# A two-layer attention, convolution and MLP trunk in split fp32: softmax scalings on VectorE, a new start condition for normalisations, and a margin ahead of attention's TensorE steps

## The chip, the cores and the metric

One NeuronCore of a Trainium2 chip runs the whole program. The metric is the device time of one execution in microseconds, as the median of several runs. TensorE has two clock levels here, 1.2 and 2.4 GHz; the profile gives the granted clock of a stretch as a share of the full one.

## The reference

Latent tokens (512) and context tokens (256) of width 1024 pass through two layers. Everything is fp32. Cut to what matters:

```python
for l in range(DEPTH):                                   # 2 layers
    h = rms_norm(x, g_norm1[l]) * (1 + sc1) + sh1        # shifts and scales: silu(c) @ w_mod + b
    na_q, na_k, na_v, cv_x, cv_b, cv_c, wa_q, wa_k, wa_v = split_proj(h @ w_in[l])
    o_na = neighborhood_attention(...)                   # 4 heads, 8 x 16 window, position bias
    o_cv = cv_b * short_conv(cv_c * cv_x, ...)           # depthwise, 3 taps
    o_wa = window_attention(...)                         # 8 heads, +-128 tokens, sink logits, rotary
    x = x + gt1 * (concat(rms_norm(o_na), rms_norm(o_cv), rms_norm(o_wa)) @ w_o[l])
    x = x + gt2 * (square(relu((rms_norm(x, g_norm2[l]) * (1 + sc2) + sh2) @ w_fc1[l])) @ w_fc2[l])
```

Both attentions are a softmax over the 256 context keys and the local keys together: `p = exp(s - max) / sum`, then `p @ v`. The context tokens go through the same steps, with a softmax over themselves, in layer 0; in layer 1 only their keys and values are needed.

## The kernel before, in words

**Tiling.** Activations lie transposed, 128 channels in the partitions and up to 768 tokens (512 latent, 256 context) along the free axis; `xs[k]` holds channels 128k to 128k+127. A product is computed to nearly fp32 by splitting each operand into a high part in fp32r and a low rest: for each step of 128 channels three matmuls add high weight times high activation, high times low and low times high into one PSUM bank `psmm` (`steps`, 526). A weight chunk arrives by DMA as `wraw`, is copied to `whi`, and the rest `wraw - whi` becomes `wlo` (`weights`, 493). In the trace `hh`/`hl` are the split activations behind a normalisation, `oh`/`ol` those of the attention outputs, `gh`/`gl` those within the MLP.

**Order.** A Python planner writes the program. Each piece of work is a generator ("stream") with a priority, run by `_Order.run` (from 280). A stream yields either a condition or a planned time, and is resumed when this has come. Each call of an engine goes through `_Engine.__getattr__` (one line, L206, which therefore stands in every row of the trace): `_cost` (209) gives a planned duration, and `_Model.op` finds the first gap in the engine's planned timetable. VectorE work whose wide operands all lie in SBUF and all GpSimd work also take a place in one common timetable called port. At the end `emit` issues all calls in order of planned start, and that is the order in which each engine does them. `quickest` (464) chooses between engines: the one with the earliest planned end plus a given penalty. `copy` chooses between ScalarE and VectorE, `minus`, `plus` and `times` between GpSimd and VectorE.

**Attention.** `attention_streams` (716) runs three streams per layer. `scores` makes logits, maxima and exponentials; `exp_norm` (698) does the exponential on ScalarE with its row sum, the reciprocal `sm` on VectorE, and then scales the probabilities `pb` (latent) or `pbc` (context) in place by `sm`, by `quickest` between GpSimd and VectorE. `transposes` (831) waits for the scaled tile by `yield md.at(pb)` and transposes it on TensorE into `pst` or `pstc`, from where `split_pt` makes `pth` and `ptl`. `products` (892) waits by `yield md.at(pth, ptl)` and multiplies with the values into `pso`. Matmuls of other streams (the remaining input projections, the output projection) fill TensorE between.

**Normalisations.** `norm` (601) computes the row statistic (`psr`, `t`, `acc`) and then, for each of the eight channel tiles, `tn` (VectorE), `hh` (ScalarE) and `hl` (VectorE). `group` (1090) does the same for an output group: `o` on VectorE, then the split into `oh` and `ol`. Ahead of each tile both wait in `room` (594) for a time that the planner finds.

Both layers run: modulation, norm, input projection with attention beside it, group normalisations, output projection, norm, fc1, squared ReLU, fc2. `x<-psmm` rows add a product to the residual. In layer 1 the second half of the program works on latent tokens in two segments of 256.

Of the kernel before, what the change touches and what calls it, by code (L numbers as in the profile page):

```python
# [10 lines left out]
AF = mybir.ActivationFunctionType  # L11
# [31 lines left out]
NBEG = (2, 3)  # L43
NTO = (2, 3)
NT = 2
SLACK = 3000.0


B_HI, B_LO, B_SM, B_SC = 100.0, 400.0, 700.0, 4000.0
NG = 18  # L50
NL, NS = 6, 3
SEM = 170.0
# [129 lines left out]
class _Engine:  # L182
# [26 lines left out]
    def _cost(self, op, n, outs, ins, k):  # L209
        if self._name == "PE":  # L210
            part, self._md.part = self._md.part, (ins[0].shape[0] > 64, outs[0].shape[0] > 32)
            c = 0.0 if part == self._md.part else 190.0
            if op == "transpose":
                return c + 109.0
            if ins[0].dtype == F32R:
                return c + max(n / 2.4 + 13.6, 110.0)
            return c + (4 * n / 2.4 if outs[0].shape[0] > 32 else 105.0)
        if self._name == "DMA":
            return outs[0].shape[0] * n * 4 / 360.0
        scalars = sum(1 for x in ins if x.shape[1:] == (1,) or list(x.shape[1:]) == [1]) if n > 1 else 0  # L220
        if self._name == "Activation":
            acc = 93.0 if k.get("accum_out") is not None else 0.0
            return (52.0 if ins[0].space == bass.MemoryType.PSUM else 93.0) + 0.8333 * n + 93.0 * scalars + acc
        if self._name == "Pool":
            return 149.0 + (2.104 if op == "tensor_tensor" else 0.9) * n
        if op == "reciprocal":
            return 69.0 + 6.25 * n
        return 69.0 + (0.52 if op == "tensor_scalar" else 1.0417) * n + 61.0 * min(scalars, 1)
# [85 lines left out]
def hybrid_trunk(ctx: ExitStack, tc: tile.TileContext, a: dict, out: bass.AP):  # L314
# [276 lines left out]
        copy(hi, t)  # L591
        minus(lo, t, hi.bitcast(F32))

    def room():

        yield md.start_of("DVE", 600.0) - 700.0

    def norm_tiles():
        return [[hp.tile([P, T], F32R, name=nm, tag="h") for _ in range(KC)] for nm in ("hh", "hl")]
# [1 line left out]
    def norm(l, which, xs, acc, hs, ls, s, seg, ready, end):  # L601

        s0, s1 = seg
        yield from row_rstd(acc, s0, s1, D)
        sh = M_SH1 if which == 0 else M_SH2
        for k in range(KC):
            yield f_mod[l, 2 * which, k // 4]
            yield from room()
            t = tmp("tn")
            b = modc[l][:, sh + k, s:s + 1]  # L610
            vec.scalar_tensor_tensor(out=t[:, s0:s1], in0=xs[k][:, s0:s1], scalar=amod[l][:, which, k, s:s + 1],
                                     in1=acc[:, s0:s1], op0=ALU.mult, op1=ALU.mult)
            act.activation(hs[k][:, s0:s1], t[:, s0:s1], AF.Identity, bias=b)
            hi = hs[k][:, s0:s1].bitcast(F32)
            vec.scalar_tensor_tensor(out=ls[k][:, s0:s1], in0=t[:, s0:s1], scalar=b, in1=hi, op0=ALU.add,
                                     op1=ALU.subtract)
            if k == 0:
                ready.set()
        if end:
            free(acc)  # L620
# [77 lines left out]
    def exp_norm(dst, src, mn, sink, tail=0):  # L698

        sm = ap_.tile([P, 2], F32, name="sm", tag="sm", bufs=6)  # L700
        act.activation(dst, src, AF.Exp, bias=mn, scale=-1.0, accum_out=sm[:, 0:1])
        if sink is not None:
            act.activation(sm[:, 1:2], sink, AF.Exp, bias=mn, scale=-1.0)
            vec.tensor_tensor(out=sm[:, 0:1], in0=sm[:, 0:1], in1=sm[:, 1:2], op=ALU.add)
        vec.reciprocal(sm[:, 0:1], sm[:, 0:1])
        w = dst.shape[1] - tail
        k = {"out": dst[:, 0:w], "in0": dst[:, 0:w], "scalar1": sm[:, 0:1], "scalar2": None, "op0": ALU.mult}
        quickest((pool, "tensor_scalar", (), k, 0.0), (vec, "tensor_scalar", (), k, B_SM))

    def split_pt(pt, n, dh, dl):  # L710
        src = pt[:, :P * n].rearrange("p (c q) -> p c q", c=dh.shape[1])
# [4 lines left out]
    def attention_streams(l, last, units, o_done):  # L716
# [114 lines left out]
        def transposes():  # L831
            pts = None
            done = 0
            while done < total:
                yield lambda: to_t
                un, j, pair, b, pb = to_t.pop(0)
                yield md.at(pb)
                if pair == 2 or b % 2 == 0:
                    yield r_pt.need()
                    r_pt.take()  # L840
                    pts = (ap_.tile([P, PTW], F32R, name="pth", tag="pth"),
                           ap_.tile([P, PTW], F32R, name="ptl", tag="ptl"))
                pth, ptl = pts
                whole = [x[:, 0:1024].rearrange("p (s q) -> p s q", s=4) for x in pts]
                half = [x[:, 1024:PTW].rearrange("p (s q) -> p s q", s=1) for x in pts]
                if pair == 2:
                    yield r_ps.need()
                    r_ps.take()
                    pt = psp.tile([P, 512], F32, name="pstc", tag="ps")
                    for c in range(2):  # L850
                        for b in range(2):
                            pe.transpose(pt[:, 256 * c + P * b:256 * c + P * b + P],
                                         pb[:, 256 * b + P * c:256 * b + P * c + P], ident)
                    split_pt(pt, 4, whole[0][:, 0:2, :], whole[1][:, 0:2, :])
                    r_ps.give(md.last(pt))
                else:

                    if un["u"] < 2:
                        parts = (([(128, 256, 384)], 0, 64), ([(0, 256, 384, 128)], 0, None),
                                 ([(0, 256, 384, 128)], 0, None), ([(0, 128, 256)], 1, 384))[b]  # L860
                        parts = [(cs, parts[1]) for cs in parts[0]] + ([parts[2]] if parts[2] is not None else [])
                    else:
                        parts = ([((256, 384, 0, 128), 0)], [((0, 128, 384, 512), 0), ((256,), 4)],
                                 [((128, 384, 512, 256), 0), ((0,), 4)], [((0, 256, 384, 128), 0)])[b]
                    qo = P * (b % 2)
                    for part in parts:
                        if isinstance(part, int):

                            pe.transpose(pt[0:64, 384:512], pb[:, part:part + 64], ident)
                            ph = 64 * pair  # L870
                            dh = pth[ph:ph + 64, 1024:PTW]
                            act.activation(dh, pt[0:64, 384:512], AF.Copy)
                            vec.tensor_tensor(out=ptl[ph:ph + 64, 1024:PTW], in0=pt[0:64, 384:512],
                                              in1=dh.bitcast(F32), op=ALU.subtract)
                            r_ps.give(md.last(pt))
                            continue
                        cs, s0 = part
                        n = len(cs)
                        yield r_ps.need()
                        r_ps.take()  # L880
                        pt = psp.tile([P, 512], F32, name="pst", tag="ps")
                        for i, c in enumerate(cs):
                            pe.transpose(pt[:, P * i:P * i + P], pb[:, c:c + P], ident)
                        split_pt(pt, n, *(half if s0 == 4 else [x[:, s0:s0 + n, qo:qo + P] for x in whole]))
                        if part is parts[-1] or not isinstance(parts[-1], int):
                            r_ps.give(md.last(pt))
                r_pb.give(md.last(pb))
                if pair == 2 or b % 2 == 1:
                    to_pv.append((un, j, pair, pth, ptl))
                    done += 1  # L890

        def products():
            for _ in range(total):
                yield lambda: to_pv
                un, j, pair, pth, ptl = to_pv.pop(0)
                yield md.at(pth, ptl)
                yield r_ps.need()
                r_ps.take()
                v, o, h0, u = un["v"][j], un["o"], 64 * j, un["u"]
# [65 lines left out]
    def main():  # L965
# [16 lines left out]
        for l in range(DEPTH):  # L982
# [107 lines left out]
            def group(gi, os_, base, n, flags, f):  # L1090
# [8 lines left out]
                for (s0, s1) in segs:  # L1099
                    yield from row_rstd(acc, s0, s1, n)  # L1100
                    for i, o in enumerate(os_):
                        if s0 == 0:
                            yield r_g.need(2)
                            r_g.take(2)
                            oh[base + i] = gp.tile([P, T], F32R, name="oh", tag="g")
                            ol[base + i] = gp.tile([P, T], F32R, name="ol", tag="g")
                        yield from room()
                        vec.scalar_tensor_tensor(out=o[:, s0:s1], in0=o[:, s0:s1], scalar=vc(V_GO + base + i),
                                                 in1=acc[:, s0:s1], op0=ALU.mult, op1=ALU.mult)
                        split(oh[base + i][:, s0:s1], ol[base + i][:, s0:s1], o[:, s0:s1])  # L1110
# [283 lines left out]
```

## Time and profile before

| | |
|---|---|
| median of 3 runs | 1689.58 us (1686.2 to 1690.01) |
| profiled execution | 1685.32 us |
| its span | 1683.5 us |
| mean granted TensorE clock | 0.986 |
| busy: TensorE, VectorE, ScalarE, GpSimd | 1590.3 (94%), 982.0 (58%), 694.9 (41%), 290.4 us (17%) |
| moved by DMA | 182.25 MB, 108 GB/s on average |

The span is the time from the first to the last instruction that the profiler recorded in one execution. Layer 0's attention lies at about 40 to 322 us and layer 1's at about 1045 to 1258 us; the rest is mostly dense products. A row that ends in `[4.57 <-DVE wlo L206]` says that the engine stood idle for 4.57 us before this instruction, and that VectorE's `wlo` ended the wait. PE is TensorE, PEld its weight loads, DVE VectorE, ACT ScalarE, POOL GpSimd.

### The profile page before, as it was taken

Reading aid. Unit: us, or ns where it says so; the run is one execution under the profiler, and the core shown is the slowest. Engines: PE = TensorE matmul, PEld = TensorE weight load, DVE = VectorE, ACT = ScalarE, POOL = GpSimd, SP = SyncE. Lnnn points to the kernel's source line nnn. Section 1 sums busy time; section 2 is a strip of 40 time slices with the busy share of each in tenths; the row PEclk is TensorE's granted clock in tenths of the full one; section 3 lists DMA queues with packets and bytes.
Section 4 is the critical chain, followed back from the end, with each engine's and each line's share of the span. In section 5 each row is a group of like instructions: output and inputs, shape, how many; then the busy total and the mean of one; then the engine's idle time right before and its main releaser. Section 6 shows DMA issues by size and latency. Waiting matters only on the chain. (4 is left out here: it accounts for less than half of the span.)

```text
span 1683.5 us, 24437 instructions
## 1 busy us (share of the span) xinstructions
PE 1590.3 (94%) x9210; PEld 1310.3 (78%) x9210; DVE 982.0 (58%) x1956; ACT 694.9 (41%) x1385; POOL 290.4 (17%) x287
## 2 busy tenths in 40 slices
PE   5999999998899999999999998988999899999999
PEld 1777778777688888888888877777778788888887
DVE  4798888855643334234334457887886754545353
ACT  3667776534431122113113345656764532323231
POOL 1034666300000000000000001356752000000000
PEclk8999999999999999999999998999999999999999
DMA  9332311245433233333321233311214322322222
GB/s 325 105 112 82 126 60 52 91 162 173 145 121 123 103 126 111 115 120 106 126 94 62 88 129 116 92 51 57 53 62 136 120 97 97 100 91 100 98 98 102
DMA packets 75719, 182.25 MB, mean 108 GB/s; under 512 B 9425, under 2 KB 15825, under 8 KB 75601
## 3 DMA queue, kind: packets, MB, share of 16 engines
q1 hardware_dynamic: 75600, 180.69, 32.7%
q8 instruction: 72, 1.18, 0.3%
q14 instruction: 47, 0.38, 0.1%
HBM read 170.43 MB, written 5.24 MB: 104 GB/s over the span
## 5 line engine op out<-in xcount | busy, mean ns | idle before, releaser
L206 PE MATMUL psmm<-hh,whi 128*128 128x512 f32 (+1 forms) x1264 | 459.5, 363 | 4.0 <-ACT hh L206 3.6
L206 PE MATMUL psmm<-hl,whi 128*128 128x512 f32 (+1 forms) x1264 | 445.1, 352 | 1.3 <-DVE hl L206 0.8
L206 PE MATMUL psmm<-hh,wlo 128*128 128x512 f32 (+1 forms) x1264 | 443.9, 351 | 0.0
L206 ACT ACTIVATE whi<-wraw 128x512 fp32r<-128x512 f32 x319 | 199.6, 629 | 442.1 <-PE psmm L206 421.0
L206 DVE TENSOR_TENSOR wlo<-wraw,whi 128x512 fp32r<-128x512 f32 x370 | 259.3, 705 | 133.1 <-ACT whi L206 129.2
L206 PE MATMUL psmm<-gh,wlo 128*128 128x512 f32 (+1 forms) x768 | 273.3, 356 | 10.3 <-DVE wlo L206 10.3
L206 PEld LDWEIGHTS psmm<-hh,whi 128*128 128x128 f32 x1264 | 240.3, 190 | 51.6 <-issue 18.5
L206 PE MATMUL psmm<-gh,whi 128*128 128x512 f32 (+1 forms) x768 | 276.4, 360 | 0.0
L206 PE MATMUL psmm<-gl,whi 128*128 128x512 f32 (+1 forms) x768 | 273.2, 356 | 0.0
L206 PEld LDWEIGHTS psmm<-hh,wlo 128*128 128x128 f32 x1264 | 240.1, 190 | 32.5 <-DVE wlo L206 0.2
L206 PEld LDWEIGHTS psmm<-hl,whi 128*128 128x128 f32 x1264 | 240.7, 190 | 30.9 <-DVE hl L206 3.6
L206 DVE SCALAR_TENSOR_TENSOR x<-psmm,modc,x 128x512 f32<-128x512 f32 (+1 forms) x96 | 63.5, 661 | 197.0 <-PE psmm L206 196.9
L206 POOL TENSOR_SCALAR pb<-pb,sm 128x512 f32<-128x512 f32 (+2 forms) x96 | 159.6, 1667 | 101.2 <-DVE sm L206 90.9
L206 PEld LDWEIGHTS psmm<-gh,wlo 128*128 128x128 f32 x768 | 146.5, 191 | 31.0 <-DVE wlo L206 10.5
L206 PEld LDWEIGHTS psmm<-gh,whi 128*128 128x128 f32 x768 | 146.5, 191 | 29.2 <-issue 10.1
L206 PEld LDWEIGHTS psmm<-gl,whi 128*128 128x128 f32 x768 | 146.5, 191 | 19.6 <-issue 0.2
L206 ACT ACTIVATE rl<-psmm 128x512 f32<-128x512 f32 (+1 forms) x98 | 50.9, 519 | 256.8 <-PE psmm L206 256.4
L206 DVE TENSOR_TENSOR sqf<-rl 128x512 f32<-128x512 f32 (+1 forms) x98 | 58.2, 594 | 156.1 <-ACT rl L206 152.8
L206 POOL TENSOR_TENSOR acc<-acc,sq 128x256 f32<-128x256 f32 x33 | 27.3, 827 | 680.8 <-ACT sq L206 680.5
L206 PE MATMUL psmm<-oh,wlo 128*128 128x256 f32 (+1 forms) x256 | 81.3, 318 | 9.6 <-DVE wlo L206 9.6
L206 PE MATMUL pst<-ident,pb 128*128 128x128 f32 (+1 forms) x416 | 64.9, 281 | 26.1 <-POOL pb L206 25.2
L206 PE MATMUL psmm<-oh,whi 128*128 128x256 f32 (+1 forms) x256 | 83.8, 327 | 3.6 <-ACT oh L206 3.6
(141 smaller groups left out, 2140.1 us busy)
## 6 DMA issues: line engine op xcount, KB each, us to landing
wraw<-in_w_fc SPq DMA_DIRECT2D x134, 512.0 KB, 3.5
wm<-in_w_mod SPq DMA_DIRECT2D x192, 256.0 KB, 4.2
wraw<-in_w_in SPq DMA_DIRECT2D x33, 512.0 KB, 3.5
wraw<-in_w_o SPq DMA_DIRECT2D x27, 512.0 KB, 3.6
tb<-in_namask SPq DMA_DIRECT2D x24, 256.0 KB, 2.8
sw<-qg SPq DMA_DIRECT2D x40, 64.0 KB, 2.0
kl<-kl SPq DMA_DIRECT2D x12, 192.0 KB, 2.6
x<-in_xT SPq DMA_DIRECT2D x8, 256.0 KB, 5.2
```

The costliest lines, as they stand in the source:

```text
L206: self._md.log.append((s, len(self._md.log), lambda: f(*a, **k)))
```

## The change

The scaling of probabilities is now chosen between VectorE, without a penalty, and ScalarE, with a penalty of 9999 ns. The planner's cost of a GpSimd `tensor_scalar` is 277 + 2.504 ns a column in place of 149 + 0.9. `room` is given the statistic's tile and asks for the first gap that the coming instruction would really have, after its input is ready, on VectorE and the port timetable, less 700 ns; before it asked for the first 600 ns gap on VectorE from the planner's present time on, less 700 ns. The two TensorE streams of attention are resumed 400 ns after their data is planned to be there.

```diff
+LATE = 400.0
...
-B_HI, B_LO, B_SM, B_SC = 100.0, 400.0, 700.0, 4000.0
+B_HI, B_LO, B_SM, B_SC, B_RM = 100.0, 400.0, 9999.0, 4000.0, 700.0
...
         if self._name == "Pool":
-            return 149.0 + (2.104 if op == "tensor_tensor" else 0.9) * n
+            return 149.0 + 2.104 * n + (128.0 + 0.4 * n if op == "tensor_scalar" else 0.0)
...
-    def room():
-
-        yield md.start_of("DVE", 600.0) - 700.0
+    def room(x):
+
+        yield md.slot("DVE", max(md.t, md.ready(x, "DVE", False)), 69.0 + 61.0 + 1.0417 * x.shape[1], [x]) - B_RM
...
-            yield from room()
+            yield from room(acc[:, s0:s1])
...
-        quickest((pool, "tensor_scalar", (), k, 0.0), (vec, "tensor_scalar", (), k, B_SM))
+        quickest((vec, "tensor_scalar", (), k, 0.0), (act, "activation", (dst[:, 0:w], dst[:, 0:w], AF.Copy),
+                                                      {"scale": sm[:, 0:1]}, B_SM))
...
-                yield md.at(pb)
+                yield md.at(pb) + LATE
...
-                yield md.at(pth, ptl)
+                yield md.at(pth, ptl) + LATE
```

The second `room` call, in `group`, is changed in the same way. Counted over the program, 120 scalings go from GpSimd to VectorE (48 of 512 columns, 32 of 640, 16 of 448, 24 of 256) and none to ScalarE; 13 `wlo` go from VectorE to GpSimd, and 36 small copies from VectorE to ScalarE. TensorE's and the DMA queue's instructions keep their number.

In layer 0's attention, VectorE's list around one unit's maxima `mn_350` and reciprocal `sm_351` before:

```order
L206 ISA pb_349,mn_350<-sc_348,wamask_111,sinks_108 128x512
L206 ISA mn_350 128x1
L206 TENSOR_TENSOR ptl_344<-pst_352,pth_343 128x4x128
L206 TENSOR_TENSOR ptl_344<-pst_353,pth_343 128x128
L206 RECIPROCAL sm_351<-sm_351 128x1
L206 TENSOR_REDUCE mnc_356<-scc_354 128x2
```

and with the change (line 206 is now 207; the numbers name the tiles):

```order
L207 ISA pb_349,mn_350<-sc_348,wamask_111,sinks_108 128x512
L207 ISA mn_350 128x1
L207 TENSOR_TENSOR ptl_344<-pst_355,pth_343 128x4x128
L207 TENSOR_TENSOR ptl_344<-pst_356,pth_343 128x128
L207 RECIPROCAL sm_351<-sm_351 128x1
L207 TENSOR_SCALAR pb_349<-pb_349,sm_351 128x512
```

The scaling of `pb_349` now stands behind the reciprocal in VectorE's own list.

At the end of layer 0, where layer 1's first normalisation (`tn`, `hl`) meets the last fc2 products of layer 0 (`x`) and the next weights, VectorE's list before:

```order
L206 SCALAR_TENSOR_TENSOR tn<-x_1146,amod_115,acc 128x512
L206 SCALAR_TENSOR_TENSOR hl<-tn,modc_113,hh 128x512 x2
L206 SCALAR_TENSOR_TENSOR tn<-x_1157,amod_115,acc 128x512
L206 SCALAR_TENSOR_TENSOR tn<-x_1168,amod_115,acc 128x512
L206 SCALAR_TENSOR_TENSOR hl<-tn,modc_113,hh 128x512 x2
L206 SCALAR_TENSOR_TENSOR x_1126<-psmm,modc_112,x_1126 128x256
L206 TENSOR_TENSOR wlo<-wraw,whi 128x512
L206 SCALAR_TENSOR_TENSOR x_1135<-psmm,modc_112,x_1135 128x256
```

and with the change:

```order
L207 SCALAR_TENSOR_TENSOR x_1132<-psmm,modc_112,x_1132 128x256
L207 TENSOR_TENSOR wlo<-wraw,whi 128x512
L207 SCALAR_TENSOR_TENSOR tn<-x_1106,amod_115,acc 128x512
L207 SCALAR_TENSOR_TENSOR x_1143<-psmm,modc_112,x_1143 128x256
L207 TENSOR_TENSOR sq<-x_1143 128x256
L207 SCALAR_TENSOR_TENSOR hl<-tn,modc_113,hh 128x512
L207 TENSOR_TENSOR wlo<-wraw,whi 128x512
L207 SCALAR_TENSOR_TENSOR x_1154<-psmm,modc_112,x_1154 128x256
L207 TENSOR_TENSOR wlo<-wraw,whi 128x512
L207 SCALAR_TENSOR_TENSOR tn<-x_1109,amod_115,acc 128x512
```

The block of pairs is broken up: weight rests and residual sums stand between `tn` and `hl`, and the later pairs come behind them.

At the end of layer 1's attention, where `o_2537` is the fourth tile of the window-attention group and `acc_2489` (now `acc_2491`) the statistic of the last group, before:

```order
L206 SCALAR_TENSOR_TENSOR t_2726<-psr_2725,t_2726 128x512
L206 SCALAR_TENSOR_TENSOR acc_2489<-t_2726,acc_2489 128x512
L206 SCALAR_TENSOR_TENSOR o_2354<-o_2354,vecs_91,acc_2489 128x512
L206 SCALAR_TENSOR_TENSOR o_2619<-o_2619,vecs_91,acc_2489 128x512
L206 TENSOR_TENSOR ol_2728<-o_2354,oh_2727 128x512
L206 TENSOR_TENSOR ol_2730<-o_2619,oh_2729 128x512
L206 SCALAR_TENSOR_TENSOR o_2537<-o_2537,vecs_91,acc_2312 128x512
```

and with the change:

```order
L207 TENSOR_TENSOR wlo_2726<-wraw_2672,whi_2725 128x512
L207 SCALAR_TENSOR_TENSOR o_2537<-o_2537,vecs_91,acc_2303 128x512
L207 TENSOR_TENSOR ol_2723<-o_2537,oh_2722 128x512
L207 TENSOR_TENSOR ocv_2731<-psmm_2724,y_2669 128x512
L207 CAST whi_2732<-wraw_2672 128x512
L207 SCALAR_TENSOR_TENSOR t_2728<-psr_2727,t_2728 128x512
L207 SCALAR_TENSOR_TENSOR acc_2491<-t_2728,acc_2491 128x512
```

The fourth tile `o_2537` stood behind the last group's whole chain and now stands ahead of it.

## Rows read from the trace of the kernel before

**Rows 1.** Windows of core 0: us, busy time of each engine, PEclk, DMA share, GB/s

```profile
40.00:322.00 282.00, 264.22 (x1744) 215.71 (x1743) 237.79 (x570) 192.95 (x443) 132.37 (x129) 1.00 0.28 90
405.00:460.00 55.00, 45.03 (x284) 36.42 (x283) 39.80 (x73) 25.11 (x47) 5.27 (x6) 0.88 0.42 142
995.00:1045.00 50.00, 38.75 (x237) 34.94 (x236) 36.96 (x64) 25.56 (x48) 5.04 (x6) 0.86 0.34 103
1045.00:1258.00 213.00, 193.45 (x1154) 160.36 (x1153) 178.25 (x418) 138.03 (x298) 116.81 (x108) 0.99 0.23 68
1258.00:1345.00 87.00, 75.20 (x531) 69.85 (x530) 64.13 (x116) 46.32 (x92) 14.17 (x16) 0.96 0.36 120
```

The engines stand in the order PE, PEld, DVE, ACT, POOL, each with its number of instructions.

**Rows 2.** Waits of TensorE, whole span: us in total, times, longest us

```profile
PE pst L206 <- POOL pb L206: 25.2, 36, 2.8
PE psmm L206 <- DVE wlo L206: 19.9, 3, 10.3
...
PE pstc L206 <- POOL pbc L206: 3.5, 8, 0.9
```

**Rows 3.** Timeline of TensorE: start us, us, instruction, idle before and releaser

```profile
416.43 0.58 PE L206 MATMUL psmm<-oh,wlo 128*128 128x256 f32 x1 [4.57 <-DVE wlo L206]
...
440.62 0.44 PE L206 MATMUL psmt<-ident,row 128*128 128x128 f32 x2 [3.40 <-DVE row L206]
...
443.05 0.79 PE L206 MATMUL psmm<-hh,whi 128*128 128x512 f32 x1 [2.00 <-ACT hh L206]
...
1016.67 0.58 PE L206 MATMUL psmm<-gh,wlo 128*128 128x256 f32 x1 [10.33 <-DVE wlo L206]
...
1270.24 0.38 PE L206 MATMUL psmm<-oh,whi 128*128 128x256 f32 x1 [3.55 <-ACT oh L206]
...
1319.31 0.39 PE L206 MATMUL psmm<-oh,wlo 128*128 128x256 f32 x1 [4.99 <-DVE wlo L206]
```

**Rows 4.** Windows behind four of these waits, columns as in the first group

```profile
416.40:422.00 5.60, 5.57 (x28) 4.54 (x29) 4.09 (x6) 0.96 (x2) 1.96 (x2) 0.51 0.69 208
443.10:449.20 6.10, 6.10 (x14) 4.44 (x15) 5.71 (x11) 3.35 (x6) 0.00 (x0) 0.50 0.00 0
1016.70:1022.70 6.00, 6.00 (x28) 6.00 (x29) 3.74 (x6) 0.77 (x3) 1.45 (x2) 0.51 0.66 182
...
1319.60:1323.00 3.40, 3.40 (x18) 3.40 (x18) 3.12 (x5) 0.84 (x2) 1.61 (x2) 0.50 0.49 162
```

**Rows 5.** Timeline of VectorE ahead of the wait at 1016.67 us

```profile
1003.52 1.41 DVE L206 SCALAR_TENSOR_TENSOR tn<-x,amod,acc 128x512 f32<-128x512 f32 x2
1005.07 1.42 DVE L206 SCALAR_TENSOR_TENSOR hl<-tn,modc,hh 128x512 fp32r<-128x512 f32 x2
1006.40 1.41 DVE L206 SCALAR_TENSOR_TENSOR tn<-x,amod,acc 128x512 f32<-128x512 f32 x2
...
1015.94 0.68 DVE L206 TENSOR_TENSOR wlo<-wraw,whi 128x512 fp32r<-128x512 f32 x1
```

**Rows 6.** Groups on GpSimd: count, busy us, mean ns of one, idle before

```profile
L206 POOL TENSOR_SCALAR pb<-pb,sm 128x512 f32<-128x512 f32 (+2 forms) x96 | 159.6, 1667 | 101.2 <-DVE sm L206 90.9
...
L206 POOL TENSOR_SCALAR pb<-pb,sm 128x512 f32<-128x512 f32 x48 | 75.8, 1582 | 47.1 <-DVE sm L206 42.9 <-PE pst L206 1.8 <-PE pso L206 1.4
...
L206 POOL TENSOR_SCALAR pbc<-pbc,sm 128x256 f32<-128x256 f32 x24 | 23.3, 980 | 6.1 <-ACT pbc L206 3.6 <-DVE ptl L206 1.2 <-DVE sm L206 0.9
...
L206 POOL TENSOR_TENSOR wlo<-wraw,whi 128x512 fp32r<-128x512 f32 x24 | 32.4, 1349 | 98.7 <-ACT whi L206 63.1 <-DVE whi L206 35.5
```

**Rows 7.** Groups on VectorE of one shape each, columns as in the sixth group

```profile
L206 DVE CAST whi<-wraw 128x512 fp32r<-128x512 f32 x75 | 33.7, 450 | 49.4 <-PE psmm L206 45.9 <-DMA wraw<-in_w_fc 1.8 <-DMA wraw<-in_w_o 0.4
...
L206 DVE TENSOR_TENSOR wlo<-wraw,whi 128x512 fp32r<-128x512 f32 x370 | 259.3, 705 | 133.1 <-ACT whi L206 129.2 <-PE psmm L206 1.6
...
L206 DVE SCALAR_TENSOR_TENSOR o<-o,vecs,acc 128x512 f32<-128x512 f32 x12 | 10.3, 873 | 0.1
```

**Rows 8.** Timeline of all engines around 1074 us

```profile
1073.56 1.63 POOL L206 TENSOR_TENSOR wlo<-wraw,whi 128x512 fp32r<-128x512 f32 x1 [20.43 <-ACT whi L206]
...
1074.07 1.68 DVE L206 TENSOR_TENSOR wlo<-wraw,whi 128x512 fp32r<-128x512 f32 x1
```

More of the change, by code (lines that the diff above doesn't have):

```diff
@@ L1106, in group @@
                             ol[base + i] = gp.tile([P, T], F32R, name="ol", tag="g")
-                        yield from room()
+                        yield from room(acc[:, s0:s1])
                         vec.scalar_tensor_tensor(out=o[:, s0:s1], in0=o[:, s0:s1], scalar=vc(V_GO + base + i),
```

## The prediction

> **What bounds the kernel now.** I read the windows first. [Rows 1] cut the span into five stretches around the two attentions and the changes of sub-layer; in the rest of the span TensorE hardly rests, so it bounds the kernel, and a change that leaves the matmuls alone can only gain where TensorE stands idle or runs at half its clock. In the two attention stretches (40 to 322 us, 1045 to 1258 us) it rests 282.00 − 264.22 = 17.8 and 213.00 − 193.45 = 19.6 us. In the three short stretches it rests 10.0, 11.3 and 11.8 us, and the granted clock falls to 0.88, 0.86 and 0.96.
>
> The list of waits then says for whom. [Rows 2]: in 36 places TensorE's transposes `pst` wait for the scaled probabilities `pb` from GpSimd, 25.2 us together, 2.8 at the longest, and `pstc` for `pbc` another 3.5 us. The 19.9 us on VectorE's `wlo` are no part of attention: three waits. The timeline of TensorE puts them and their neighbours in place [rows 3]: site A at 416 to 443 us (4.57 on `wlo`, 3.40 on `row`, 2.00 on `hh`), site B at 1016.67 us (10.33 on `wlo`), site C at 1270.24 us (3.55 on `oh`), site D at 1319.31 us (4.99 on `wlo`). A..D are the ends of attention groups and the starts of normalisations.
>
> Each such idle time is followed by a stretch with a granted clock of 0.50 or 0.51, which is 1.2 GHz, half of the full 2.4: 5.60, 6.10, 6.00 and 3.40 us [rows 4]; the 3.40 us occur three times (after sites C and D, and once at 1080.7 us after an attention wait). Work done at half the clock takes twice as long, so each costs half its length: 2.8, 3.05, 3.0 and 1.7 us.
>
> Why `wlo` is late at B stands in VectorE's timeline [rows 5]: from 1003.52 us it does two `tn`, two `hl`, two `tn`, and so on, eight pairs wall to wall, and only at 1015.94 the `wlo` for which TensorE has stopped. The normalisation has pushed the weight splitting aside.
>
> **The scalings.** The change moves 120 in-place scalings from GpSimd to VectorE, and none to ScalarE. On GpSimd they take 159.6 + 23.3 = 182.9 us, 1582 ns for 512 columns [rows 6]. The trace has no such operation on VectorE. The nearest rows bound it [rows 7]: a plain `CAST` of 128x512 takes 450 ns, the normalisation's `o`, with a scalar and two whole tensors, 873 ns. A scaling has the scalar, but only one tensor, so it lies nearer the cast: I take 0.55 us. The chain from scores to `pst` then shrinks by about 1 us. The mean wait is 25.2/36 = 0.7 us, and TensorE's transposes and products are now planned 0.4 us later than their data, with other matmuls ahead of them. Most waits go; the long ones, up to 2.8 us, leave something. Of 25.2 + 3.5 = 28.7 us and the 1.7 us of half clock at 1080.7 I leave 9 and count **−21.4 us**. Bounds: nothing left (−30.4), or twice as much left (−12.4).
>
> **VectorE's load.** The scalings have 48·512 + 32·640 + 16·448 + 24·256 = 58,368 columns, 114 times 512: 114 × 0.55 = 62.7 us (51 at the cast's price, 99.5 at that of `o`). The order shows 13 `wlo` going from VectorE to GpSimd (13 × 0.705 = 9.2 us by [rows 7]) and 36 small copies from VectorE to ScalarE (at most 0.45 each, 16 us). Net some +38 us, bounds 26 and 75. VectorE's free time in the attention stretches is 282.00 − 237.79 = 44.2 and 213.00 − 178.25 = 34.7 us, 78.9 together [rows 1]. So it fits, by little at the upper bound: I cost it at **0**, covered by that free time; without it the whole excess would land on TensorE. GpSimd's 13 more `wlo` at 1349 ns [rows 6] are 17.5 us on an engine that loses 182.9: nothing. ScalarE's copies lie in its own 89 and 75 us of free time: nothing.
>
> One row speaks against that cover [rows 8]: a `wlo` on VectorE that began at 1074.07 us, while GpSimd was within its own `wlo` (1073.56 to 1075.19), took 1.68 us in place of 0.705. VectorE stood still until GpSimd had finished. After the change GpSimd keeps about 132.37 + 116.81 − 182.9 + 17.5 = 84 of the 495 us of both stretches, 17%. If every scaling that meets it (120 × 0.17 = 20) waits half a GpSimd operation (0.67 us), that is 14 us more of VectorE time, still inside the 78.9 us. The Trainium skill, page "SBUF — State Buffer", section "Who interferes with whom", gives the rule: VectorE's copies, casts and scalings in their two-port mode, and its operations with two SBUF inputs, share a port pair with GpSimd; whoever comes first locks it for a whole instruction and the other blocks. The trace agrees with it (1.68 us). By the rule alone the moved scalings become blockable, which is the first rival below; by the row's price it does not change the sum.
>
> **The normalisations.** The new condition plans each `tn` or `o` at its true place on VectorE and, by the change's order, sets weight splits and the residual sums `x` between the pairs (site B), and lets the fourth tile of another group go ahead of the last group's chain (site C). The `wlo` waits at A, B, D and the `oh` wait at C are caused by blocks of this kind. At stake: A 4.57 + 3.40 + 2.00 + 2.8 + 3.05 = 15.8; B 10.33 + 3.0 = 13.3; C 3.55 + 1.7 = 5.3; D 4.99 + 1.7 = 6.7; together 41.1 us. What is late next: the last `hh` and `hl` pairs, now behind other work, and the first matmuls of the next product wait for them. Two pairs take 2.88 us (1003.52 to 1006.40, [rows 5]); I charge that once at each of A, B and D, 8.6 us. **−32.5 us**. Bounds: −41.1, and −24 if the charge doubles.
>
> **Sum.** 1685.3 (the profiled execution's own time) − 21.4 − 32.5 = 1631.4 us. That execution is 4.3 us below the median of the runs shown, so the forecast is 1635.7, **1636 us**. With all bounds at their best end 1618; the 8.6 us of other small waits in the attention stretches (37.4 − 28.7) could bring 1610. With both at their worst end 1653.
>
> **Rivals.**
> 1. VectorE takes GpSimd's place. It is busy 84% of both stretches now, and (237.79 + 178.25 + 38)/495 = 92% afterwards; a scaling that queues behind `ptl`, `wlo` or a GpSimd lock is as late as before. For: 92%, [rows 8]. Against: GpSimd's scaling is three times as long as mine, and the 0.4 us margin. The waits of 28.7 us stay under another name: 1685.3 − 32.5 + 4.3 = 1657 us.
> 2. The normalisations give back what they gain: with work between, `hh` and `hl` come late, and TensorE waits at the same sites for ScalarE and VectorE instead of for `wlo`, followed by the same half clock. For: 2.00 us on `hh` at A already. Against: at B the block runs ahead of what TensorE needs. 1685.3 − 21.4 + 4.3 = 1668 us. Both rivals together mean that the change doesn't do what it says: 1690 us, no change.
> 3. Slower: the in-place scaling on VectorE is no cheaper than on GpSimd. Then VectorE takes 182.9 − 9.2 − 16 = 158 us more, 79 over its free time, and becomes the bound in attention: 1685.3 − 32.5 + 79 + 4.3 = 1736 us. The excess exceeds the sites' gain from (78.9 + 32.5 + 25.2)/114 = 1.2 us for 512 columns. Against: no elementwise VectorE row in [rows 7] comes near.
>
> **Chances.** Forecast (1618 to 1653) 0.72, rival 1 0.12, rival 2 0.07, both together 0.05, rival 3 0.04. A measurement of this kernel can tell some 0.3%, 5 us, from no change. Faster 0.72 + 0.12 + 0.07 = 0.91, same 0.05, slower 0.04. The range takes in the forecast's bounds, 1610, rival 1 and most of the way to rival 2: 1610 to 1664, leaving out about 0.16.
>
> **What would show it.** Right: `pb` scalings on VectorE at 0.45 to 0.87 us for 512 columns; no `pst` wait on GpSimd and under 10 us on whatever replaces it; TensorE's rest in the two attention stretches down from 37 to some 17 us; at B `wlo` between the pairs and the 10.33 us gone; fewer stretches at 0.50. Wrong: `pst` waits of over 20 us on VectorE (rival 1), new waits of over 3 us on `hh`, `hl` or `oh` after the sites (rival 2), scalings over 1.2 us (rival 3).

## The result, and the profile after

The change makes the kernel faster: 1645.79 us (median of 4 runs, 1644.47 to 1646.77) against 1688.98 us, a ratio of 0.9746 with a 95% interval of 0.9729 to 0.9763. The forecast was 1636 us, range 1610 to 1664. The gain is 43.2 us where 53 were expected. Between the two profiled executions it is 38.5 us (span 1683.5 to 1645.0); the rest is that the profiled execution of before stands 3.7 us below its median and that of after 1.0 above.

To see where the time went I cut both traces at the same six matmuls: the first input projection of layer 0 (`hh`), its first output projection (`oh`), its first fc1, the first input projection of layer 1, its first output projection, and the first fc2 of layer 1. The windows of before at these cuts, with the columns of [rows 1]:

```profile
31.92:346.20 314.28, 296.50 (x1944) 239.32 (x1943) 256.82 (x600) 204.59 (x468) 140.79 (x138) 0.99 0.31 102
346.20:430.24 84.04, 79.47 (x475) 63.68 (x473) 48.25 (x80) 33.19 (x58) 7.69 (x9) 0.96 0.53 176
430.24:1027.78 597.54, 581.81 (x3485) 483.00 (x3483) 251.73 (x446) 154.86 (x277) 7.07 (x9) 0.98 0.33 110
1027.78:1265.45 237.67, 217.20 (x1266) 179.61 (x1265) 196.28 (x451) 153.19 (x326) 118.09 (x109) 0.99 0.24 70
1265.45:1374.88 109.43, 97.64 (x632) 88.79 (x630) 74.51 (x135) 51.28 (x100) 12.89 (x15) 0.97 0.36 120
```

and those of after:

```profile
31.03:333.14 302.11, 294.77 (x1971) 240.63 (x1969) 267.48 (x645) 207.48 (x477) 45.56 (x69) 1.00 0.35 111
333.14:414.44 81.30, 79.47 (x475) 62.27 (x473) 49.05 (x85) 35.20 (x63) 12.55 (x14) 0.98 0.53 178
414.44:993.34 578.90, 575.69 (x3459) 479.30 (x3457) 243.80 (x434) 152.12 (x273) 7.17 (x7) 1.00 0.33 111
993.34:1231.22 237.88, 220.66 (x1266) 184.46 (x1265) 213.97 (x487) 162.14 (x348) 53.43 (x71) 0.97 0.24 71
1231.22:1336.32 105.10, 98.51 (x631) 89.16 (x630) 74.33 (x137) 50.60 (x99) 12.02 (x14) 0.97 0.39 125
```

Read down the lengths: layer 0's attention is 12.2 us shorter, its output projection 2.7, the MLP with the step to layer 1 18.6, layer 1's output projection and fc1 4.3. In layer 0's attention TensorE's rest (length less busy time) falls from 17.8 to 7.3 us. **Layer 1's attention stretch is as long as before** (237.67 and 237.88 us). TensorE still rests 17.2 us there (20.5 before), at a lower clock (0.97 for 0.99), and VectorE is busy for 213.97 of 237.88 us, 90%.

The scalings on VectorE, by groups of one shape, against [rows 6]:

```profile
L207 DVE TENSOR_SCALAR pb<-pb,sm 128x512 f32<-128x512 f32 x48 | 24.2, 503 | 1.6
...
L207 DVE TENSOR_SCALAR pb<-pb,sm 128x640 f32<-128x640 f32 x32 | 18.5, 577 | 1.1
...
L207 DVE TENSOR_SCALAR pbc<-pbc,sm 128x256 f32<-128x256 f32 x24 | 8.5, 356 | 1.2
L207 DVE TENSOR_SCALAR pb<-pb,sm 128x448 f32<-128x448 f32 x16 | 7.7, 484 | 0.6
```

503 ns for 512 columns, a third of GpSimd's 1582, and 58.9 us in all. TensorE's waits after, whole span, against [rows 2]:

```profile
PE psmm L207 <- ACT hh L207: 4.3, 6, 2.2
PE psmm L207 <- DVE wlo L207: 3.6, 6, 1.4
...
PE pst L207 <- DVE pb L207: 0.8, 3, 0.4
```

The 28.7 us on GpSimd are 0.8 on VectorE, and the 19.9 us on `wlo` are 3.6. But in layer 1's attention alone the list of after has new names, each once or twice:

```profile
PE psmm L207 <- ACT whi L207: 2.2, 1, 2.2
PE sc L207 <- DVE ptl L207: 1.8, 1, 1.8
PE pso L207 <- DVE ptl L207: 1.8, 2, 1.0
...
PE pso L207 <- ACT pth L207: 1.4, 1, 1.4
PE psr L207 <- ACT qg L207: 1.4, 1, 1.4
```

The first is no wait of attention. It stands at 996.51 us, behind the first three matmuls of layer 1's input projection, and is what is left of site B (see below). Behind it TensorE runs at half clock:

```profile
998.50:1001.70 3.20, 3.20 (x9) 2.46 (x8) 2.76 (x5) 2.34 (x5) 0.00 (x0) 0.50 0.49 164
```

So some 2.15 + 1.6 = 3.8 us of layer 1's attention stretch belong to site B; before, all of B lay ahead of the cut.

Another wait can be followed in the timeline of all engines at 1216 us:

```profile
1216.12 1.83 DVE L207 SCALAR_TENSOR_TENSOR o<-o,vecs,acc 128x512 f32<-128x512 f32 x1
1216.12 1.28 POOL L207 TENSOR_TENSOR wlo<-wraw,whi 128x512 fp32r<-128x512 f32 x1 [0.78 <-ACT whi L207]
...
1217.98 0.63 ACT L207 ACTIVATE oh<-o 128x512 fp32r<-128x512 f32 x1 [1.94 <-DVE o L207]
1218.51 0.77 ACT L207 ACTIVATE pth<-pst 128x384 fp32r<-128x384 f32 x2
...
1219.04 0.39 PE L207 MATMUL pso<-pth,vst 128*128 128x256 f32 x1 [1.40 <-ACT pth L207]
1220.45 0.58 PE L207 MATMUL pso<-ptl,vst 128*128 128x256 f32 x1 [1.03 <-DVE ptl L207]
```

VectorE's `o` takes 1.83 us where its mean is 0.835; a `wlo` on GpSimd starts at the same moment. ScalarE's `oh` waits for it, `pth` stands behind `oh`, and TensorE waits 1.40 and 1.03 us. The Trainium skill, page "SBUF — State Buffer", section "Who interferes with whom", states the lock of the port pair shared with GpSimd; this row agrees (1.83 us for 0.835). Behind these two waits the clock falls:

```profile
1220.40:1226.90 6.50, 6.45 (x19) 5.34 (x20) 6.18 (x11) 2.28 (x4) 0.00 (x0) 0.50 0.00 0
```

6.50 us at a granted clock of 0.50, 1.2 GHz: by the prediction's count another 3.2 us lost.

### The profile page after: what moved, and what is told of

It is laid out like the page before. It is cut to its first block, busy times and chain, and to the rows that moved or that the text cites. A ratio compares the mean times of both kernels' runs of the same rounds, so it can differ in the third digit from the quotient of the medians.

```text
span 1645.0 us, 24426 instructions
## 1 busy us (share of the span) xinstructions
PE 1586.5 (96%) x9210; PEld 1311.4 (80%) x9210; DVE 1002.1 (61%) x2030; ACT 705.9 (43%) x1415; POOL 135.3 (8%) x183
## 4 chain that ended last, share of the span: by engine, by line
PE 67%; DVE 14%; ACT 5%; issue 3%; DMA 2%; POOL 0%; SPq 0%; DVEq 0%; ACTq 0%; POOLq 0%
PE psmm L207 61%; DVE pb L207 3%; PE psm L207 2%; DVE ptl L207 2%; ACT pb L207 1%; PE pso L207 1%; DVE o L207 1%; PE pst L207 1%; DVE wlo L207 1%; PE sc L207 1%; DVE hl L207 1%; DVE t L207 1%; DVE sm L207 1%; PE psr L207 1%; DVE tn L207 1%
## 5 line engine op out<-in xcount | busy, mean ns | idle before, releaser
L207 ACT ACTIVATE whi<-wraw 128x512 fp32r<-128x512 f32 x323 | 202.9, 630 | 426.2 <-PE psmm L207 403.3
L207 DVE TENSOR_TENSOR wlo<-wraw,whi 128x512 fp32r<-128x512 f32 x357 | 246.9, 694 | 127.5 <-ACT whi L207 124.0
L207 ACT ACTIVATE pb<-pb,mn 128x513 f32<-128x513 f32 (+3 forms) x96 | 72.1, 752 | 62.8 <-DVE mn L207 57.0
L207 PE MATMUL psmm<-ol,whi 128*128 128x256 f32 (+1 forms) x256 | 79.8, 312 | 0.0
```

The source lines that it names most:

```text
L207: self._md.log.append((s, len(self._md.log), lambda: f(*a, **k)))
```

## The experiments

Each run has its ratio to the kernel before on the same chip; the kernel before took 1685.27 to 1688.98 us on the chips used, so runs are compared by their ratios. "Attention 0" and "attention 1" are the lengths of the two layers' attention stretches between the same matmuls as above, from each run's trace.

| run | scalings | start condition | margin, ns | us | ratio (95% interval) | attention 0, us | attention 1, us |
|---|---|---|---|---|---|---|---|
| before | GpSimd | old | 0 | 1688.98 | 1 | 314.3 | 237.7 |
| e1 | VectorE | old | 0 | 1677.02 | 0.9937 (0.9917 to 0.9957) | 317.9 | 234.6 |
| e2 | GpSimd | new | 0 | 1676.75 | 0.9927 (0.9902 to 0.9952) | 313.2 | 243.4 |
| e3 | GpSimd | old | 400 | 1680.55 | 0.9959 (0.9943 to 0.9976) | 317.8 | 234.3 |
| e4 | VectorE | new | 0 | 1659.92 | 0.9830 (0.9808 to 0.9852) | 316.2 | 240.6 |
| e5 | VectorE | old | 400 | 1662.95 | 0.9864 (0.9838 to 0.9889) | 304.3 | 233.6 |
| e8 | GpSimd | new | 400 | 1669.56 | 0.9900 (0.9875 to 0.9925) | 316.8 | 241.9 |
| after | VectorE | new | 400 | 1645.79 | 0.9746 (0.9729 to 0.9763) | 302.1 | 237.9 |
| e6 | half ScalarE | new | 400 | 1660.13 | 0.9844 (0.9822 to 0.9867) | 312.7 | 239.5 |
| e7 | VectorE | new | 800 | 1660.12 | 0.9847 (0.9826 to 0.9867) | 308.5 | 246.3 |
| e9 | VectorE, 16 columns | new | 400 | 1629.26 | 0.9660 (0.9639 to 0.9681) | 294.0 | 226.9 |
| e10 | GpSimd, true price | new | 400 | 1660.65 | 0.9845 (0.9825 to 0.9866) | 307.6 | 242.7 |
| e11 | VectorE | new | 400, transposes only | 1671.50 | 0.9906 (0.9888 to 0.9923) | 316.7 | 247.3 |
| e12 | VectorE | new | 300 | 1662.38 | 0.9851 (0.9833 to 0.9870) | 316.6 | 239.4 |

**e1, the scalings alone.** From the changed kernel:

```diff
-LATE = 400.0
+LATE = 0.0
...
-            yield from room(acc[:, s0:s1])
+            yield from room()
```

with the old `room`. 

> The kernel before with the scalings on VectorE alone: old start condition of the normalisations, margin 0. The theory of the prediction (the scaling pays by itself for the waits on GpSimd): about 21 us less than before, 1668 us, with some 9 us of waits left in both attentions. The theory that VectorE is too full in layer 1's attention: 9 to 12 us less, 1678 us, all of it in layer 0, the stretch from layer 1's first input projection to its first output projection as long as before (237.7 us). The theory that the scaling needs the margin: no change, since TensorE's order then asks for the transposes earlier, and the same waits stand under VectorE's name.

Measured: 10.6 us less (0.0063 × 1689). In the profiled execution the gain is not where I put it: layer 0, from its first input projection to that of layer 1, is 995.5 us long against 995.9 before; attention 1 is 3.1 us shorter. No wait on `pb` is among its larger ones, but

```profile
PE psmm L207 <- DVE wlo L207: 26.6, 5, 10.3
```

stands in place of 19.9 us [rows 2]. In the two attentions together TensorE's rest falls from 38.3 to 30.4 us, but its busy time rises by 8.4 us, with a granted clock of 0.98 for 0.99 in layer 0. The first theory is refuted, the second has the size but not the place, the third not the size.

**e2, the start condition alone** (`B_SM`, the two ways and the price of `exp_norm` as before, `LATE = 0.0`). 

> The kernel before with the new start condition of the normalisations alone: scalings on GpSimd, margin 0. The theory of the prediction: 32 us less at most, about 1657 us, the 10.33 us wait on wlo gone and waits of some 2 us on hh in its place. If the stretches of the two traces are right, 2.7 + 18.6 + 4.3 = 26 us less, 1663 us. The rival that the two parts help each other at the sites (GpSimd is free for wlo only when the scalings are gone) gives under 15 us less, over 1674 us.

Measured: 12.3 us less, 1676.75, as the rival said (over 1674). Layer 0 gained 14.7 us (981.2 for 995.9), attention 1 lost 5.7 and layer 1's output projection with fc1 3.0.

**e3, the margin alone** (400 ns in the kernel before). 

> The kernel before with the margin of 400 ns alone. The theory that the margin hides waits: the mean wait for GpSimd was 0.7 us, so about half of the 28.7 us goes and 10 to 14 us are gained, 1677 us. The theory that it costs (tiles are held longer, the products come later): 0 to 10 us slower. The prediction gave it no price of its own.

Measured: 6.9 us less, between the gain of 10 to 14 us and the loss that the two theories said.

**e4, the changed kernel without the margin.**

```diff
-LATE = 400.0
+LATE = 0.0
```

> The changed kernel with the margin at 0. If the margin is what takes layer 1's gain back, this is faster than the changed kernel, 1635 to 1640 us. If it hides waits, this is slower, 1650 to 1656 us, with transposes pst waiting for pb on VectorE. If VectorE's load is the cause, within 3 us of 1646, and layer 1's attention stretch still about 238 us.

Measured: 1659.92, a little more than the second theory said. The waits of `pst` on VectorE that it named are small (2.6 us on `pb`); so the size fits and the reason does not. By the stretches the margin's 14 us stand in layer 0's attention, 316.2 us without it and 302.1 with it (the other stretches together cancel):

```profile
31.57:347.75 316.18, 302.99 (x1969) 242.58 (x1968) 277.14 (x653) 208.62 (x480) 46.45 (x72) 0.98 0.33 105
```

**e5, the old start condition in the changed kernel.**

```diff
-            yield from room(acc[:, s0:s1])
+            yield from room()
```

> The changed kernel with the old start condition of the normalisations: scalings on VectorE and the margin of 400 ns. If the parts add, 11 + 7.4 us less than before, 1670 us. If margin and scalings need each other in attention (the margin gains 14 us on top of the other two parts, 7.4 alone), 1662 to 1666 us. The waits on wlo at the ends (some 20 to 27 us) stay in either case.

Measured: 1662.95, within the second theory's range; the parts do not add. Layer 0's attention is nearly as short as in the changed kernel:

```profile
30.97:335.31 304.34, 296.96 (x1968) 241.12 (x1967) 266.57 (x640) 209.26 (x481) 46.34 (x69) 0.99 0.34 111
```

The waits on `wlo` stay as foretold:

```profile
PE psmm L207 <- DVE wlo L207: 27.2, 7, 10.3
```

**e6, every second scaling on ScalarE.**

```diff
+        n_sm[0] += 1
-        quickest((vec, "tensor_scalar", (), k, 0.0), (act, ...
+        quickest((vec, "tensor_scalar", (), k, 0.0 if n_sm[0] % 2 else 19999.0), (act, ...
```

> The changed kernel with every second scaling on ScalarE: some 30 us of VectorE time less over both attentions, 15 in layer 1's. If VectorE's load (214 of 238 us) is what keeps layer 1's attention at 238 us, that stretch falls below 232 us and the whole to 1636 to 1641 us. If latency along the chain of each unit is, ScalarE being slower per column, no change or slower, 1645 to 1652 us.

Measured: 1660.13, and it does not answer the question: VectorE's busy time in attention 1 is 213 us, as in the changed kernel, since the planner filled the place (13 `wlo` came back from GpSimd, for one).

**e7, twice the margin** (`LATE = 800.0`). 

> The changed kernel with the margin doubled to 800 ns. If the waits left in layer 1's attention (17 us) are executions that run behind the planned times, more margin takes some of them away: 1636 to 1642 us. If VectorE's load is the limit, no change within 4 us. If tiles held longer cost, slower, over 1650 us.

Measured: 1660.12, with attention 1 at 246.3 us. The third theory has the sign, though layer 0 is only 3.8 us longer than with 400 (966.1 for 962.3), and its attention keeps 7.7 of the 14.1 us that 400 ns gain there over none.

**e8, the scalings back on GpSimd** (`B_SM`, the two ways and GpSimd's planned price in `exp_norm` as before). 

> The changed kernel with the scalings back on GpSimd (new start condition and margin stay). If the parts add, 42 - 11 = 31 us less than before, 1657 us. If the margin does most in attention, 1650 us. If the start condition needs a free GpSimd and VectorE's place for the scalings, 1665 to 1670 us.

Measured: 1669.56, the third theory. The margin does not hide GpSimd:

```profile
PE pst L207 <- POOL pb L207: 24.8, 37, 2.1
```

**e9, VectorE's load without a change of order.** The planner charges the full scaling, the instruction that is issued does 16 columns and leaves the others unscaled:

```diff
         def call(*a, **k):
+            short = k.pop("short", None)
             s = self._md.op(self._name, *self._parse(op, a, k))
+            if short:
+                k = dict(k, out=k["out"][:, 0:short], in0=k["in0"][:, 0:short])
...
-        getattr(eng, op)(*a, **k)
+        getattr(eng, op)(*a, **(dict(k, short=16) if eng is vec and op == "tensor_scalar" else k))
```

> The changed kernel with every instruction in its place on every engine, but each scaling does 16 columns in place of its 256 to 640; the other probabilities stay unscaled. That takes some 50 us of VectorE time out of the two attentions and leaves the order alone. If VectorE's load is what TensorE still waits for in layer 1's attention, that stretch (237.9 us, 17.2 idle) falls to 225 to 230 and the whole to 1632 to 1638 us. If the load is covered by VectorE's free time, as the prediction counted it (0), within 4 us of 1646.

Its scalings by groups, and its windows for the two attentions:

```profile
L210 DVE TENSOR_SCALAR pb<-pb,sm 128x16 f32<-128x16 f32 x96 | 25.2, 263 | 3.3
L210 DVE TENSOR_SCALAR pbc<-pbc,sm 128x16 f32<-128x16 f32 x24 | 6.2, 258 | 1.2
```

```profile
31.65:325.61 293.96, 290.46 (x1971) 240.60 (x1969) 253.88 (x645) 206.72 (x477) 44.71 (x68) 1.00 0.36 114
...
984.36:1211.27 226.91, 214.76 (x1266) 181.33 (x1265) 201.39 (x486) 160.34 (x346) 52.01 (x71) 0.99 0.25 75
```

Measured: 58.9 − 31.4 = 27.5 us less in the scalings on VectorE, less than I had said, and 1629.26 us, 16.5 below the changed kernel (14.5 by the ratios). Both attentions shorten, by 8.1 and 11.0 us. This is the clearest run of all: nothing was moved, so the scalings' time on VectorE reaches TensorE, some 0.5 to 0.6 us of the whole for each microsecond taken off them. Part may be the shorter chain of each unit (scaling, transpose, product) rather than the load. TensorE waited for `pb` itself only 0.8 us; and of its rest in attention 1, which falls from 17.2 to 12.2 us, some 2.2 us were waits of `psr` for `qg` and `sqq`, which no scaled tile goes into. That part points to the load; the rest the run does not part.

**e10, GpSimd at its true price** (the two ways of before in `exp_norm`, the new price, `B_SM` at 9999). 

> The changed kernel with the scalings on GpSimd, planned at the price that they really have there (277 + 2.504 ns a column); start condition and margin stay. If the waits for GpSimd came from the planner's too low price alone (149 + 0.9 ns), the move to VectorE was not needed: 1644 to 1650 us, pst waits under 8 us. If GpSimd is too slow in attention whatever the plan, 1660 to 1672 us.

Measured: 1660.65, at the second theory's lower end, though the waits fell:

```profile
PE pst L207 <- POOL pb L207: 10.5, 8, 2.7
```

Against e8 the true price alone is worth 9 us by the ratios and more than halves the waits (24.8 to 10.5); layer 0's attention is 9.2 us shorter. Of the 26 us between e8 and the changed kernel, 17 are left for VectorE.

**e11, the margin ahead of the transposes only.**

```diff
-                yield md.at(pth, ptl) + LATE
+                yield md.at(pth, ptl)
```

> The changed kernel with the margin ahead of the transposes alone, none ahead of the products. If the margin works because the transposes asked too early for the scaled tiles, most of the 14 us stays: 1646 to 1650 us. If it is the products, that wait for ptl on VectorE, 1656 to 1660 us, as with no margin.

Measured: 1671.50, far over both, with products that wait for VectorE:

```profile
PE pso L207 <- DVE ptl L207: 9.3, 9, 2.3
```

**e12, a margin of 300 ns.** 

> The changed kernel with a margin of 300 ns. If the margin covers a lateness of a few hundred ns, 1646 to 1652 us. If 400 is a lucky order among many (0 and 800 both gave 1660), it falls back to 1655 to 1660 us.

Measured: 1662.38. Margins of 0, 300, 400 and 800 ns give 1660, 1662, 1646 and 1660, as the second theory said of the whole. In layer 0's attention they give 316.2, 316.6, 302.1 and 308.5 us: there 800 ns keep half of the gain and lose it in layer 1's (246.3).

## Why the prediction was right, and where it was not

- **The bound and the sign.** TensorE's idle time was the place to look. From 93.2 us of the span (1683.5 − 1590.3) it fell to 58.5 (1645.0 − 1586.5), and its busy time by 3.8. The stretches at half clock are not fewer, as the prediction had it: behind the start of the program six before and six after (windows of 0.5 us), 37 and 27.5 us together. And not all of the rest of the span is dense: ahead of layer 0's first input projection TensorE rests 19.1 of 31.92 us, which the change leaves as it is (18.5 of 31.03).
- **The scaling's price** was right: 0.55 us taken, 0.503 measured; 62.7 us in all, 58.9 measured. Rival 3 is out.
- **"I cost it at 0, covered by that free time"** is the step that failed. The net load was smaller than the +38 us charged (VectorE's busy time rose by 20.1 us, from 982.0 to 1002.1), and still it was not covered: VectorE is busy 89 and 90% of the two attentions, and shortening the scalings by 27.5 us is worth 14.5 to 16.5 us (e9). TensorE's order hangs there on VectorE's next `ptl` or `o`. The attention term, −21.4, measured −12.2 + 0.2 = −12.0 by the stretches; it is −15.8 if site B's 3.8 us are taken out of layer 1's, and some 1.5 more, since modulation matmuls `psm` of 1.5 us moved into layer 0's attention. So rival 1 holds in part: the waits on GpSimd are gone, and by e9 both attentions pay for VectorE, layer 1's more.
- **The sites** are the other term that was too large: −32.5 expected, −2.7 − 18.6 − 4.3 = −25.6 measured, or −21.9 with B's 3.8 us, outside the bound of −24. The charge of 8.6 us held the new waits but not the half clock behind them. No new wait is over 3 us, so rival 2 holds in that part only. At B the mechanism is as foretold: 10.33 us on `wlo` became 0.67. What is late next has the size that I charged (2.15 us for 2.88), but not the name: the fourth matmul of layer 1's input projection waits for its weights `whi`, not for `hh` or `hl`. The timeline of TensorE at that place:

```profile
992.04 0.39 PE L207 MATMUL psmm<-gh,wlo 128*128 128x256 f32 x1 [0.67 <-DVE wlo L207]
...
996.51 0.50 PE L207 MATMUL psmm<-hh,whi 128*128 128x512 f32 x1 [2.15 <-ACT whi L207]
```

  and of ScalarE ahead of the second row:

```profile
995.83 0.63 ACT L207 ACTIVATE whi<-wraw 128x512 fp32r<-128x512 f32 x1 [0.44 <-DMA wraw<-in_w_in]
```

  The copy ends at 996.46 us; ScalarE's idle time before it was ended by the transfer of the weights. At D it is `hh`, as charged, with 6.5 us at half clock behind it:

```profile
1293.52 0.38 PE L207 MATMUL psmm<-hh,whi 128*128 128x256 f32 x1 [2.17 <-ACT hh L207]
```

```profile
1295.50:1302.00 6.50, 5.87 (x23) 5.11 (x24) 4.99 (x11) 2.46 (x6) 0.00 (x0) 0.50 0.00 0
```

  C and D kept 4.3 of the 9 us expected.
- **The sum** treated the parts as independent. Alone they give 10.6, 12.3 and 6.9 us, 29.8 together; as a whole 42.9. Taken out of the whole, they cost 26, 20 and 14 us (ratios of e8, e5 and e4 less that of after, times 1689). With GpSimd's scalings the start condition gains 5.3 and 8.3 us in layer 0's output projection and MLP and gives back 8.7 in layer 1 (e2); with the scalings alone the waits on `wlo` stay (e1). How the one part brings about the other's loss is not shown.
- **The margin** had no price of its own in the prediction, which counted it among the reasons why most waits go. It does not hide GpSimd's waits (24.8 us in e8), and the whole gains its 14 us at 400 ns alone. The gain lies in layer 0's attention and does not come from the margin alone: with VectorE's scalings and the margin 302.1 us (304.3 with the old start condition, e5), without the margin 316.2 and 317.9 (e4, e1), with the margin and GpSimd's scalings 316.8 and 317.8 at their old planned price (e8, e3) and 307.6 at the true one (e10). So it is not one lucky order; but 300 ns give nothing there, and why 400 suits and 300 does not stays open. A third of the whole gain thus hangs on a constant that the prediction did not price: without it the time would have been 1660 us (e4), still within the range but nearer to rival 1's 1657 than to the forecast.
- The forecast missed by 10 us: 9.4 in attention and 6.9 at the sites (5.6 and 10.7 with B's 3.8 us counted to its site), less 0.9 gained in the start and 5.3 between the profiled executions and the medians.

No run that leaves no work out is faster than the changed kernel.

## What to carry to other kernels

Free time on an engine covers new work only if that engine is not also the next link of the chain that the bounding engine waits for; at 90% busy, as here, charge the work, and test it by shortening the instruction without moving it (e9). A constant that a planner turns into another order of the whole program has to be tried at several values before its effect is called a mechanism: here 300 ns gives nothing and 400 gives 14 us; and by stretches, since a gain in one (800 ns, layer 0's attention) can be lost in another. Where a planner's price for an operation is wrong (610 ns planned, 1582 measured), correct the price first and see what is left for the change of engine.

## What the runs showed of the hardware that was not expected

An `o` on VectorE that starts together with a GpSimd operation took 1.83 us in place of 0.835; the cost reached TensorE two engines later, and as half clock for 6.50 us. A scaling of 16 columns takes 263 ns on VectorE where one of 512 takes 503: about half of the time did not depend on the length.
